# The first gate pair by seven products, with its weights on GpSimd's queue, in a one-layer encoder kernel

## The chip, the cores and the metric

The kernel runs on one core of one Trainium2 chip. The metric is the device time of one execution in microseconds (us). Before the change the median of three runs is 776.86 us, from 776.81 to 778.23. TensorE (PE) multiplies matrices, ScalarE (ACT) and VectorE (DVE) work element by element, GpSimd (POOL) does so too, and issues transfers from its own queue; SyncE (SP) only issues transfers. Each engine takes its instructions strictly in the order in which the program lists them, and an instruction waits on semaphores for what other engines and transfers must have done.

## The reference

One layer over x (512 positions of 1024 features, fp32):

```python
n = rms_norm(h, norm_mix_pre)
proj = n @ w_in                    # columns: gMLP u | gMLP v | q | k | v | gates A, B (1024 each)
y_a = u * (W_s LN(v) + b_s)        # gelu first; 4 chunks of 128 positions, 4 groups of 128 features
y_b = dilated_window_attention(q, k, v)    # 3 patterns x 4 heads, mixed by their denominators
merged = sigmoid(gate_A) * (y_a @ w_branch_a) + sigmoid(gate_B) * (y_b @ w_branch_b)
h = h + rms_norm(merged @ w_out, norm_mix_post)
h = h + rms_norm(relu(rms_norm(h) @ w_up)**2 @ w_down, norm_mlp_post)
```

Everything is fp32. The change lies between y_a and merged @ w_out.

## The kernel before

**Products.** A factor is split into a high part (hi, rounded to the type that TensorE multiplies fast) and a low part (lo, what the rounding left out). One product of 128x128 by 128xN is three matmuls: hi by hi, hi by lo, lo by hi. The usual split is a ScalarE copy for hi and a VectorE subtraction for lo (`wsplit`, L68; `split_into`, L86). The other way is `dma_split` (L78): ScalarE writes hi and then minus hi into the low's tile, and GpSimd issues an accumulating transfer that adds the original weights from memory onto it.

**Seven products.** `seven` and `seven_pairs` (L344 to L390) compute a pair of 128 gate columns for both gates, over 1024 inputs and 512 positions, as a 2x2 block product by seven smaller products instead of eight, each of 12 matmuls of 128x256: 84 matmuls. `seven` forms the sums of the weight blocks on VectorE and splits them; `nmov` holds the sums of the activations, made earlier. The seventh of them, product 4, is deferred as `tail` and stands in the next pair. The same pair written plainly is 2 x 8 products of 128x512, 48 matmuls.

**Stages, in order.** Norm and the V0 projection; V1 and V2; for four heads the q and k projection by seven products and attention (`mix`, heads 0 to 2 store their result to `ybd` in memory, L647); the gMLP: v with LayerNorm per chunk (`evac_v`, L690), and for each of four groups g the u features (`pf`, 24 matmuls of 128x512), the spatial product of that group (`pg`, L727) with the four normalized chunks `vln` and the transposed spatial weights `wst`, and y_a. `prs` (L686) is the sum over `wst` for the LayerNorm bias. `ybh` and `ybl` are loaded back from `ybd` at L659, on GpSimd's queue. LayerNorm's reciprocal root is a power on GpSimd (`rs_out`, L104), one for each chunk, and VectorE applies it (`vln`, L702).

Then the gates and branches, for d from 0 to 7: weights `gw` (1 MB for a pair) and branch weights `bw` (two of 256 KB), gates by sigmoid, then `branches` (L790): y_b by w_branch_b (b1) and y_a by w_branch_a (b0), 12 matmuls of 128x512 each, times the gates, summed, and split into `mh` and `ml`, block d of w_out's input. `GSTD = 1`: pair 0 is written plainly (L802 to L807), pairs 1 to 7 by seven products. After that w_out (`pd`, L849 to L909): its eight blocks k are loaded two at a time (`wow`) into one raw ring of three buffers which the first up weights (`upw`) use next; two pre copies split the first up weights. Then norm, up and down.

**What sets the order.** The code is written stage by stage, but the order of each engine's instructions is set at build time by a scheduler which plays the program through with a cost model of its own and puts what it thinks ready first. So a new buffer or another queue can move instructions that the diff does not name. On a queue nothing overtakes: a transfer that waits holds up all that stands behind it on its engine.

**Memory.** Tiles lie in pools, opened and closed like a stack. A pool that is opened on memory of a closed one waits for that one's last readers. `gpool` holds the gMLP's tiles and `gapool` the gate stage's.

## Time and profile before

| | |
|---|---|
| median of 3 runs | 776.86 us |
| the profiled execution | 776.86 us |
| its span, first to last instruction | 775.1 us |
| mean granted clock of TensorE | 0.999 |
| busy: TensorE, its weight loads, VectorE, ScalarE, GpSimd | 766.0, 691.2, 604.4, 463.9, 88.0 us |
| moved by DMA | 130.40 MB, 168 GB/s in the mean |

Rows of a timeline give the start in us, the duration in us, the engine, the line of the code, the operation and "output<-inputs"; in square brackets stands how long the engine had been idle before and what released it. A matmul's duration is longer than the step to the next one, since matmuls are pipelined; what a matmul costs is the step. In a list of waits the columns are the total, the number and the longest, in us. A row of transfers gives the queue, the number, the size and the median time from issue to landing. A row of stretches gives for each engine its busy time and in brackets its instructions, then TensorE's clock, the share of DMA and GB/s; the engines stand in the order PE, PE's weight loads, DVE, ACT, POOL.

### The profile page before, as it was taken

The numbers are of one execution on the slowest core, as the hardware profiler recorded it, in microseconds if no ns is written. First come the engines' busy times: TensorE is split into PE (matmuls) and PEld (weight loads), VectorE is DVE, ScalarE is ACT, GpSimd is POOL, SyncE is SP. The second block draws the span as 40 slices with busy tenths as digits, with TensorE's granted clock in tenths as the row PEclk, the third lists the DMA queues.
The fourth block names the chain that finished last, engine by engine and source line by source line (L and its number), as shares of the span: only waits on it lengthen the run. The fifth ranks groups of instructions, "written<-read, shape, count | busy, mean of one in ns | idle before, by whom it ended". The sixth has DMA issues, their size and how long they took to land.

```text
span 775.1 us, 12382 instructions
## 1 busy us (share of the span) xinstructions
PE 766.0 (99%) x4859; PEld 691.2 (89%) x4859; DVE 604.4 (78%) x974; ACT 463.9 (60%) x755; POOL 88.0 (11%) x125
## 2 busy tenths in 40 slices
PE   8999999999999999999999999999999999999996
PEld 5888999999998889999998899999999988888885
DVE  7884689888883878768756559998888699978785
ACT  6351468978778545445444457566666766655671
POOL 3310200010103300000000210011211100203010
PEclk9999999999999999999999999999999999999999
DMA  9733743262548933434536324469998998979803
GB/s 310 250 115 109 213 109 110 55 164 82 142 160 154 233 88 84 109 82 120 147 144 217 135 82 136 160 195 290 204 265 221 240 309 313 193 248 216 217 1 109
DMA packets 108910, 130.40 MB, mean 168 GB/s; under 512 B 3330, under 2 KB 79394, under 8 KB 107955
## 3 DMA queue, kind: packets, MB, share of 16 engines
q1 hardware_dynamic: 83920, 83.50, 34.1%
q0 software_dynamic: 24640, 45.70, 25.7%
q8 instruction: 38, 0.62, 0.3%
q10 hardware_dynamic: 290, 0.40, 0.1%
q14 instruction: 22, 0.17, 0.1%
HBM read 119.63 MB, written 26.74 MB: 189 GB/s over the span
## 4 chain that ended last, share of the span: by engine, by line
PE 97%; issue 1%; DMA 0%; DVE 0%; POOL 0%; ACT 0%; POOLq 0%; DVEq 0%; ACTq 0%
PE pacc L1011 13%; PE pg L361 12%; PE pd L1103 6%; PE pd L1102 6%; PE pd L1104 6%; PE pgacc L361 6%; PE ptp L1011 5%; PE pf L93 5%; PE pf L92 5%; PE pf L94 5%; PE pv L94 4%; PE pv L93 4%; PE pv L92 4%; PE pgS L361 3%; PE pd L94 2%; PE pd L92 2%
## 5 line engine op out<-in xcount | busy, mean ns | idle before, releaser
L1103 PE MATMUL pd<-hl,hhl 128*128 128x512 f32 x224 | 87.1, 389 | 0.0
L1104 PE MATMUL pd<-hl,hhl 128*128 128x512 f32 x224 | 87.0, 389 | 0.0
L1102 PE MATMUL pd<-hl,hhl 128*128 128x512 f32 x224 | 84.7, 389 | 0.0
L1011 PE MATMUL pacc<-nt,hl 128*128 128x256 f32 x504 | 66.1, 279 | 0.0
L1011 PEld LDWEIGHTS pacc<-nt,hl 128*128 128x128 f32 x504 | 61.9, 188 | 0.1
L74 ACT ACTIVATE hi<-s 128x1024 fp32r<-128x1024 f32 x32 | 33.8, 1059 | 29.5 <-DVE s L348 7.9
L1104 PEld LDWEIGHTS pd<-hl,hhl 128*128 128x128 f32 x224 | 42.0, 188 | 8.8
L1102 PEld LDWEIGHTS pd<-hl,hhl 128*128 128x128 f32 x224 | 42.0, 188 | 8.8
L1103 PEld LDWEIGHTS pd<-hl,hhl 128*128 128x128 f32 x224 | 42.0, 188 | 8.6
L75 DVE TENSOR_TENSOR lo<-s,hi 128x1024 fp32r<-128x1024 f32 x32 | 39.0, 1223 | 9.8 <-ACT hi L74 9.6
L87 ACT ACTIVATE hl<-s 128x1024 fp32r<-128x1024 f32 x28 | 29.4, 1057 | 26.1 <-DVE s L994 18.8
L88 DVE TENSOR_TENSOR hl<-dnw,hl 128x1024 fp32r<-128x1024 f32 x32 | 38.4, 1221 | 8.3 <-ACT hl L87 8.3
L87 ACT ACTIVATE hl<-dnw 128x1024 fp32r<-128x1024 f32 x32 | 33.0, 1053 | 19.2 <-DMA dnw<-in_w_down_dram 9.9
L1011 PE MATMUL pacc<-n,hl 128*128 128x256 f32 x336 | 44.1, 279 | 0.0
L1011 PEld LDWEIGHTS pacc<-n,hl 128*128 128x128 f32 x336 | 41.3, 188 | 0.0
L361 PE MATMUL pg<-nt,hi 128*128 128x256 f32 x216 | 39.8, 281 | 0.0
L88 DVE TENSOR_TENSOR hl<-s,hl 128x1024 fp32r<-128x1024 f32 x28 | 34.2, 1221 | 5.2 <-ACT hl L87 5.2
L92 PE MATMUL pf<-nh,hi 128*128 128x512 f32 x96 | 38.0, 396 | 0.0
L93 PE MATMUL pf<-nl,hi 128*128 128x512 f32 x96 | 37.7, 392 | 0.0
L94 PE MATMUL pf<-nh,lo 128*128 128x512 f32 x96 | 37.6, 391 | 0.0
L93 PE MATMUL pv<-lo,nh 128*128 128x512 f32 x96 | 37.4, 390 | 0.0
L92 PE MATMUL pv<-hi,nh 128*128 128x512 f32 x96 | 37.3, 395 | 0.0
(386 smaller groups left out, 2269.9 us busy)
## 6 DMA issues: line engine op xcount, KB each, us to landing
upw<-in_w_up_dram SPq DMA_DIRECT2D x16, 1024.0 KB, 6.1
qkw<-in_w_in_dram SPq DMA_DIRECT2D x24, 512.0 KB, 5.2
dnw<-in_w_down_dram SPq DMA_DIRECT2D x12, 1024.0 KB, 6.9
gw<-in_w_in_dram SPq DMA_DIRECT2D x16, 512.0 KB, 5.2
t3d<-in_w_down_dram POOLq DMA_DIRECT2D x8, 1024.0 KB, 8.5
t1d<-in_w_down_dram POOLq DMA_DIRECT2D x8, 1024.0 KB, 9.6
slab<-in_w_in_dram SPq DMA_DIRECT2D x6, 1024.0 KB, 10.6
tsum<-in_w_down_dram POOLq DMA_DIRECT2D x6, 1024.0 KB, 9.7
```

The costliest lines, as they stand in the source:

```text
L74: nc.scalar.activation(hi, raw, AF.Copy)
L75: (sub or nc.vector).tensor_tensor(lo, raw, hi.bitcast(F32), op=ALU.subtract)
L87: nc.scalar.activation(hi, src, AF.Copy)
L88: return sub.tensor_tensor(lo, src, hi.bitcast(F32), op=ALU.subtract)
L92: nc.tensor.matmul(ps, ah, bh, start=start, stop=False)
L93: nc.tensor.matmul(ps, ah, bl, start=False, stop=False)
L94: return nc.tensor.matmul(ps, al, bh, start=False, stop=stop)
L361: nc.tensor.matmul(ps, a[:, j], b[:, j], start=first and not (j or i), stop=(j == KH - 1 and i == 2), skip_group_check=True)
L1011: ins = nc.tensor.matmul(ps, a[:, j], b[:, j], start=first and not (j or m), stop=(j == KH - 1 and m == 2), skip_group_check=True)
L1102: nc.tensor.matmul(ps, ah, bh, start=start, stop=False, skip_group_check=True)
L1103: nc.tensor.matmul(ps, ah, bl, start=False, stop=False, skip_group_check=True)
L1104: return nc.tensor.matmul(ps, al, bh, start=False, stop=stop, skip_group_check=True)
```

## The change

Pair 0 goes through `seven_pairs` as well (`GSTD = 0`). For it the three plain weight blocks (`ar0`, `a12`, `ar1`) are split first, by `dma_split` with their own 256 KB rows of w_in, and its products come in the order 1, 2, 6, 5, 7, 3, so that those that need only plain blocks stand ahead of those that need sums. `gapool` is opened ahead of the close of the gMLP's pool, on the memory of attention, so that its tiles do not share memory with the gMLP's. The loads of `bw` move from SyncE's queue to GpSimd's, and the lows of both branch weights come by `dma_split`: a second ScalarE copy and an accumulating transfer on GpSimd instead of a subtraction on VectorE. `gapool` stays open beyond w_out, whose blocks from k=3 on are split into its tiles, each into one that a gate step has done with: k=3 into `ar0` and `a12`, k=4 into `bw` and `ar1`, k=5 into `b1` and `b0`, k=7's low into `gs`; the pool of w_out's own tiles shrinks from five to three.

```diff
--- before.py
+++ after.py
@@ -75,9 +75,10 @@
         (sub or nc.vector).tensor_tensor(lo, raw, hi.bitcast(F32), op=ALU.subtract)
         return hi, lo
 
-    def dma_split(raw, src):
-        hi = wpool.tile(list(raw.shape), F32R, name="hi", tag="whi")
-        lo = wpool.tile(list(raw.shape), F32R, name="lo", tag="wlo")
+    def dma_split(raw, src, hi=None, lo=None):
+        if hi is None:
+            hi = wpool.tile(list(raw.shape), F32R, name="hi", tag="whi")
+            lo = wpool.tile(list(raw.shape), F32R, name="lo", tag="wlo")
         nc.scalar.activation(hi, raw, AF.Copy)
         nc.scalar.activation(lo, hi.bitcast(F32), AF.Copy, scale=-1.0)
         nc.gpsimd.dma_start(lo, src, accum_op=ALU.add)
@@ -341,14 +342,19 @@
     by_r = perm[:, 2 * P:2 * P + 4].unsqueeze(1).unsqueeze(1)
     by_c = perm[:, 2 * P + 4:2 * P + 8].unsqueeze(1).unsqueeze(3)
 
-    def seven(raw, sums, split2, split1):
+    def seven(raw, sums, split2, split1, first=False):
         raw = raw.rearrange("p (j h) (r c) -> p j (h r) c", h=2, r=2)
+        if first:
+            plain = [split1(raw[:, :, i], tag, i) for i, tag in ((1, "ar0"), (3, "a12"), (2, "ar1"))]
         s = sums()
         nc.vector.tensor_tensor(s[:, :, 0:4:2], raw[:, :, 1:3], raw[:, :, 0:1].to_broadcast([P, KH, 2, P]), op=ALU.add)
         nc.vector.tensor_tensor(s[:, :, 3], s[:, :, 2], raw[:, :, 1], op=ALU.add)
         s12 = split2(s[:, :, 2:4])
-        ar = [split1(raw[:, :, 1], "ar0"), split1(raw[:, :, 2], "ar1")]
-        a12 = split1(raw[:, :, 3], "a12")
+        if first:
+            ar, a12 = plain[::2], plain[1]
+        else:
+            ar = [split1(raw[:, :, 1], "ar0"), split1(raw[:, :, 2], "ar1")]
+            a12 = split1(raw[:, :, 3], "a12")
         nc.vector.tensor_tensor(s[:, :, 1], s[:, :, 3], raw[:, :, 3], op=ALU.add)
         s34 = split2(s[:, :, 0:2])
         pick = lambda g, i: [z[:, :, i] for z in g]
@@ -366,17 +372,22 @@
             c2, c1 = rows(i)
             w = weights(i)
             Y, Z, X = banks()
-            product(6, Y, w, moving, True)
+            p1, z5, u2, u3 = snap("p1", two), snap("z5", 1), snap("u2", 1), snap("u3", 1)
             if tail:
+                product(6, Y, w, moving, True)
                 tail()
             product(1, X, w, moving, True)
-            p1, z5, u2, u3 = snap("p1", two), snap("z5", 1), snap("u2", 1), snap("u3", 1)
             nc.scalar.activation(p1, X, AF.Copy)
+            if not tail:
+                product(2, X, w, moving, False)
+                evac(i, c1[:, A], X)
+                product(6, Y, w, moving, True)
             nc.vector.tensor_tensor(u2, Y, p1, op=ALU.add)
             product(5, Z, w, moving, True)
             nc.scalar.activation(z5, Z, AF.Copy)
-            product(2, X, w, moving, False)
-            evac(i, c1[:, A], X)
+            if tail:
+                product(2, X, w, moving, False)
+                evac(i, c1[:, A], X)
             product(7, Y, w, moving, False)
             nc.vector.scalar_tensor_tensor(u3, Y, -1.0, p1, op0=ALU.mult, op1=ALU.subtract)
             product(3, Z, w, moving, False)
@@ -732,16 +743,16 @@
             split_into(yah[:, g], yal[:, g], tf)
 
     attn.close()
+    gp = ExitStack()
+    gapool = pool(gp, "gapool")
+    gst.close()
     mst = ExitStack()
     mpool = pool(mst, "mpool")
     mh = mpool.tile([P, KD, S], F32R, name="mh")
     ml = mpool.tile([P, KD, S], F32R, name="ml")
-    gp = ExitStack()
-    gst.close()
-    gapool = pool(gp, "gapool")
     gs, rawb = {}, {}
 
-    GSTD = 1
+    GSTD = 0
 
     w7 = w_down.rearrange("(c j h p) d -> c h p j d", p=P, h=2, j=4)
     halves = [slice(0, 512), slice(512, 1024)]
@@ -765,14 +776,23 @@
         raw = wload([KD, 2, P], lambda r: [(r[:, :, 1 - br], fcols(w_in, COL_G + br * D + d * P, KD, P)) for br in range(2)], "gw")
         rawb[d] = gapool.tile([P, 2, 4, P], F32, name="bw")
         for br, w in enumerate((w_branch_a, w_branch_b)):
-            nc.sync.dma_start(rawb[d][:, br], w[:, d * P:(d + 1) * P].rearrange("(k p) c -> p k c", p=P))
+            nc.gpsimd.dma_start(rawb[d][:, br], w[:, d * P:(d + 1) * P].rearrange("(k p) c -> p k c", p=P))
 
         return raw
 
     def gate_weights(i):
         raw = gate_raw(i + GSTD)
+
+        def added(src, tag, blk):
+            hl = gapool.tile([P, 2, KH, P], F32R, name=tag)
+            c0 = COL_G + (1 - blk % 2) * D
+            rows = w_in[:, c0:c0 + P].rearrange("(j h p) c -> h p j c", p=P, h=2)
+            dma_split(src, rows[blk // 2], hl[:, 0], hl[:, 1])
+            return hl[:, 0], hl[:, 1]
+
         with nullcontext() if i else tc.issue_after(normed[-1].ins):
-            return seven(raw.rearrange("p k r c -> p k (r c)"), wsum, wsplit, lambda src, tag: split1(src, tag, gapool))
+            return seven(raw.rearrange("p k r c -> p k (r c)"), wsum, wsplit,
+                         lambda src, tag, blk=0: added(src, tag, blk) if not i else split1(src, tag, gapool), not i)
 
     def gate_banks():
         return [psA.tile([P, 512], F32, name="pg" + tag, tag=tag, bufs=nb)[:, A] for tag, nb in (("acc", 4), ("acc", 4), ("S", 2))]
@@ -791,7 +811,7 @@
         g = gs.pop(d)
         for br in (1, 0):
             bhl = gapool.tile([P, 2, 4, P], F32R, name=f"b{br}")
-            split_into(bhl[:, 0], bhl[:, 1], rawb[d][:, br])
+            dma_split(rawb[d][:, br], fcols((w_branch_a, w_branch_b)[br], d * P, 4, P), bhl[:, 0], bhl[:, 1])
             yh, yl = ((yah, yal), (ybh, ybl))[br]
             pb = feature_tile(bhl[:, 0], bhl[:, 1], 4, yh, yl, "Ty"[br])
             nc.vector.tensor_tensor(g[:, 1 - br], pb, g[:, 1 - br], op=ALU.mult)
@@ -807,7 +827,6 @@
         branches(d)
     seven_pairs(KD - GSTD, gate_weights, nmov, gate_banks, lambda nm, nb: gapool.tile([P, 256], F32, name=nm, bufs=nb), 1,
                 gate_rows, gate_evac, gate_after)
-    gp.close()
     front.close()
     right.close()
 
@@ -849,13 +868,19 @@
             nc.vector.scalar_tensor_tensor(dst[:, hs], ys[hf], r, res[:, hs], op0=ALU.mult, op1=ALU.add)
 
     wo = ExitStack()
-    wopool = pool(wo, "wopool", bufs=5)
+    wopool = pool(wo, "wopool", bufs=3)
+    homes = iter([gapool.tile([P, D], F32R, name="wo", tag=tag) for tag in ("ar0", "a12", "bw", "ar1", "b1", "b0")]
+                 + [wopool.tile([P, D], F32R, name="wo", tag="wo") for _ in range(3)] + [gapool.tile([P, D], F32R, name="wo", tag="gs")])
     accs = [[psB.tile([P, 512], F32, name="pd", tag=tg, bufs=4) for _ in range(2)] for tg in ("acc",) * 4]
     wos, early = [], []
     for k0 in range(0, KD, 2):
         raw = wload([2, D], lambda r: [(r, w_out[k0 * P:(k0 + 2) * P].rearrange("(k p) c -> p k c", p=P))], "wow")
         for j in range(2):
-            wos.append(wsplit(raw[:, j]) if k0 + j < 3 else wsplit(raw[:, j], wopool, tag="wo"))
+            if k0 + j < 3:
+                wos.append(wsplit(raw[:, j]))
+            else:
+                wos.append((next(homes), next(homes)))
+                split_into(*wos[-1], raw[:, j])
     raw = wload([KD, 2 * P], lambda r: [(r, fcols(w_up, 0, KD, 2 * P))], "upw")
     for j in range(2):
         hl = prepool.tile([P, 2, KD, P], F32R, name="pre", tag="pre")
@@ -918,6 +943,7 @@
     wo.close()
     rst.close()
     mst.close()
+    gp.close()
     wstack.close()
 
     wback = pool(back, "wback", bufs=5)
```

The built program has 84 matmuls of 128x256 in the place of 48 of 128x512, 4800 rows of TensorE against 4764. At two places the order changes in a way that the diff does not tell.

GpSimd at the end of attention and the start of the gMLP, before: `rs_out_2949`, `_2963`, `_2977`, `_2991` are the LayerNorm powers of chunks 0 to 3, `lo_3161` and `lo_3207` the accumulating transfers of the u features of groups 2 and 3.

```order
L83 DMA lo_3161<-in_w_in_dram 128x8x128
L104 TENSOR_TENSOR rs_out_2949<-rs_in_2947,neghalf_66 128x1
L659 DMA ybh_2802<-ybd_108 128x3x512
L659 DMA ybl_2803<-ybd_108 128x3x512
L104 TENSOR_TENSOR rs_out_2963<-rs_in_2961,neghalf_66 128x1
L83 DMA lo_3207<-in_w_in_dram 128x8x128
L104 TENSOR_TENSOR rs_out_2977<-rs_in_2975,neghalf_66 128x1
L104 TENSOR_TENSOR rs_out_2991<-rs_in_2989,neghalf_66 128x1
```

The same place of the change, with what follows on GpSimd (`bw_3271` and `bw_3388` are the branch weights of pairs 0 and 1).

```order
L84 DMA lo_3161<-in_w_in_dram 128x8x128
L670 DMA ybh_2802<-ybd_108 128x3x512
L670 DMA ybl_2803<-ybd_108 128x3x512
L105 TENSOR_TENSOR rs_out_2949<-rs_in_2947,neghalf_66 128x1
L105 TENSOR_TENSOR rs_out_2963<-rs_in_2961,neghalf_66 128x1
L105 TENSOR_TENSOR rs_out_2977<-rs_in_2975,neghalf_66 128x1
L84 DMA lo_3207<-in_w_in_dram 128x8x128
L105 TENSOR_TENSOR rs_out_2991<-rs_in_2989,neghalf_66 128x1
L779 DMA bw_3271<-in_w_branch_a_dram 128x4x128
L779 DMA bw_3271<-in_w_branch_b_dram 128x4x128
L84 DMA ar0_3274<-in_w_in_dram 128x4x128
L84 DMA a12_3278<-in_w_in_dram 128x4x128
```

The power of chunk 0 stood ahead of the two loads and stands behind them now; the transfers of the gate stage follow behind the last power, where before there was none. On TensorE the first `pg` stays right behind `prs` and ahead of group 1's u features.

ScalarE at the start of w_out, before: `hi_4596` is the high part of w_out's block 2, the next ones of blocks 3 to 7, `gs_4315` the sum of the last pair.

```order
L74 ACTIVATE hi_4596<-wow_4594 128x1024
L786 ACTIVATE gs_4315<-gs_4315,cols_65 128x256
L787 ACTIVATE gs_4315<-gs_4315,cols_65 128x512
L87 ACTIVATE mh_3259<-gs_4315 128x512
L74 ACTIVATE hi_4600<-wow_4594 128x1024
L74 ACTIVATE hi_4606<-wow_4604 128x1024
L74 ACTIVATE hi_4610<-wow_4604 128x1024
L74 ACTIVATE hi_4616<-wow_4614 128x1024
L74 ACTIVATE hi_4620<-wow_4614 128x1024
L87 ACTIVATE pre_4626<-upw_4624 128x1024
L87 ACTIVATE pre_4629<-upw_4624 128x1024
```

The same place of the change: `hi_4686` is block 2, `wo_4662` and `wo_4664` are blocks 6 and 7 (3 to 5 stand earlier), `gs_4392` the sum of the last pair.

```order
L74 ACTIVATE hi_4686<-wow_4684 128x1024
L806 ACTIVATE gs_4392<-gs_4392,cols_65 128x256
L88 ACTIVATE wo_4662<-wow_4698 128x1024
L88 ACTIVATE wo_4664<-wow_4698 128x1024
L807 ACTIVATE gs_4392<-gs_4392,cols_65 128x512
L88 ACTIVATE pre_4706<-upw_4704 128x1024
L88 ACTIVATE pre_4709<-upw_4704 128x1024
L88 ACTIVATE mh_3263<-gs_4392 128x512
```

The last `mh` stood third behind block 2 and ahead of the other blocks; it stands now behind all blocks and behind both copies of the up weights. On TensorE the first 22 matmuls of w_out, of two banks, use no part of the last `mh`; the 23rd does.

## The prediction

> **What bounds the kernel now.** I read the page's head and its chain first, then the list of waits on TensorE, and after that the timelines of the two places where the order of work changes.
>
> ```profile
> span 775.1 us, 12382 instructions
> PE 766.0 (99%) x4859; PEld 691.2 (89%) x4859; DVE 604.4 (78%) x974; ACT 463.9 (60%) x755; POOL 88.0 (11%) x125
> PE   8999999999999999999999999999999999999996
> ...
> PE 97%; issue 1%; DMA 0%; DVE 0%; POOL 0%; ACT 0%; POOLq 0%; DVEq 0%; ACTq 0%
> ...
> PE pt L200 <- DVE xn L196: 1.6, 2, 1.3
> PE idle L168 <- POOL neghalf L60: 1.0, 1, 1.0
> PE pv L93 <- DVE w0lo L215: 0.2, 1, 0.2
> ```
>
> TensorE is busy for 766.0 of 775.1 us, 97% of the chain is TensorE itself, and the list of its waits has three rows, 2.8 us in all, on lines of the opening norm and V projection. From the first head to the end no matmul waits for anyone. So the time is the sum of the start-to-start steps of the matmuls: a matmul saved is worth its step, and any new wait of TensorE is paid whole. The profiled execution is the median of the runs (776.86 us, 1.8 above its span), so I add to 776.86.
>
> **The matmuls.** The first gate pair's 48 plain 128x512 products run here from the first to the start of the next pair's product; twelve branch matmuls of 128x512, then twelve 128x256 of a seven-product step, run near the end; the last row covers six whole pairs.
>
> ```profile
> 284.40 0.48 PE L92 MATMUL pf<-nh,hi 128*128 128x512 f32 x1
> ...
> 295.38 0.40 PE L361 MATMUL pgacc<-nt,hi 128*128 128x256 f32 x2
> ...
> 403.42 0.28 PE L361 MATMUL pgacc<-nh,hi 128*128 128x256 f32 x1
> ...
> 404.85 0.40 PE L92 MATMUL pf<-yah,b 128*128 128x512 f32 x1
> ...
> 407.60 1.56 PE L361 MATMUL pgacc<-nt,ar 128*128 128x256 f32 x12
> 409.00 0.39 PE L92 MATMUL pd<-hi,mh 128*128 128x512 f32 x1
> ...
> 311.00:405.00 94.00, 94.00 (x650) 87.61 (x649) 68.38 (x107) 44.56 (x78) 0.15 (x2) 1.00 0.42 121
> ```
>
> The 48 take 295.38 - 284.40 = 10.98 us, 0.229 each; twelve of 128x512 take 2.75 us, also 0.229; twelve of 128x256 take 1.43 or 1.40, 0.118 each. Seven products are 84 of the small ones: 84 x 0.118 = 9.9 us. The six pairs give the other bound: 94.0 / 6 = 15.67 us a pair, less 24 x 0.229 = 5.50 for the branches, leaves 10.17 for the 84. The saving is 0.8 to 1.1 us; I take **-0.9**.
>
> **What ScalarE and VectorE gain and lose.** Each branch low loses a VectorE subtraction (0.69 us for 128x512, the ml row below) and gets a second ScalarE copy (0.63, the mh row below) and a GpSimd transfer: 19 copies, 12 us, on ScalarE, about 11 us off VectorE. By the row of six pairs ScalarE works 44.56 and VectorE 68.38 us of 94, so two copies a pair (1.25 of 15.67) fit; I cost them at nothing. The low now takes 0.63 for the copy, then a DMA, against 0.69 before. What hides this is the lead: in the new GpSimd order the b1 low of a pair is issued ahead of the b0 low of the pair before, the better part of 15.67 us early. Without that cover it would cost some us in each of seven pairs.
>
> **First stall: GpSimd at the gMLP.** The change opens the gate pool earlier and hangs new transfers on GpSimd, and the order there is new: both loads of ybh and ybl now stand ahead of the power that makes LayerNorm's scale for chunk 0 (rs_out). What this does is to be seen on chunk 1, which stands behind them already. GpSimd, VectorE and TensorE before:
>
> ```profile
> 257.11 1.25 POOL L104 TENSOR_TENSOR rs_out<-rs_in,neghalf 128x1 f32<-128x1 f32 x1
> 261.78 0.81 POOL L659 DMA_DIRECT2D ybh<-ybd  x1 [3.42 <-DMA ybd<-yb]
> 262.58 0.76 POOL L659 DMA_DIRECT2D ybl<-ybd  x1
> 263.36 0.57 POOL L104 TENSOR_TENSOR rs_out<-rs_in,neghalf 128x1 f32<-128x1 f32 x1
> ...
> 258.39 0.55 DVE L702 TENSOR_SCALAR vln<-vln,mv,rs_out 128x512 f32<-128x512 f32 x1 [0.26 <-POOL rs_out L104]
> ...
> 263.97 0.55 DVE L702 TENSOR_SCALAR vln<-vln,mv,rs_out 128x512 f32<-128x512 f32 x1 [2.54 <-POOL rs_out L104]
> ...
> 262.68 0.38 PE L727 MATMUL pg<-wst,vln 128*128 128x128 f32 x2
> ...
> ybd<-yb POOLq DMA_DIRECT2D x1, 512.0 KB, 7.2
> ...
> ybd<-yb POOLq DMA_DIRECT2D x3, 512.0 KB, 9.0
> ...
> ybd<-yb POOLq DMA_DIRECT2D x1, 512.0 KB, 10.4
> ```
>
> The ybh load waited 3.42 us for the last head's store to ybd to land, at 261.7, and everything behind it on GpSimd waited too: chunk 1's power ran at 263.36 and its vln at 263.97, with VectorE idle for 2.54 us. TensorE did not notice, as it needs chunk 0 first, at 262.68, and that had been normalized at 258.39. Now chunk 0 takes chunk 1's place: power 263.36 to 263.93, vln 263.97 to 264.52, and TensorE's first pg, still in its old place right behind prs, starts at 264.56 instead of 262.68: **+1.9 us**. Queued behind that pg are all matmuls of the second u feature. The last rows are the first store's time to landing, the median of the three, and the last one's, which counts here. GpSimd's order is unchanged up to it, so I keep its 10.4 us; at 9.0 the stall would be 0.5, at 7.2 nothing. Bounds 0 and 1.9. The later chunks move by the same 1.9 on TensorE as on VectorE, so I add nothing for them.
>
> **Pair 0's lows.** The first low (ar0, 256 KB, added by DMA) stands on GpSimd behind the two bw loads of its pair, and these wait for the last py, since the pool lies on attention's old memory.
>
> ```profile
> 268.56 0.39 PE L640 MATMUL py<-ptb,v12s 128*128 128x128 f32 x2
> ...
> 277.25 1.05 PE L727 MATMUL pg<-wst,vln 128*128 128x128 f32 x8
> 278.06 0.48 PE L92 MATMUL pf<-nh,hi 128*128 128x512 f32 x1
> ...
> DMA to landing us min/median/max: 3.2/5.7/7.2
> ...
> DMA to landing us min/median/max: 6.3/8.5/9.9
> ```
>
> The last py ends at 268.95, so at 270.8 with the first stall. Two issues of 0.8 us (as ybh's) put ar0's at 272.4. Product 1 stands in the new order where 278.06 is here, 280.0 with the stall, and needs its low two matmuls on. So 7.8 us are to be had. The nearest rows lie on both sides: plain 256 KB loads of v12s on this queue took 3.2 to 7.2 (first row), accumulating 512 KB loads 6.3 to 9.9 (second). I take 0, as half the bytes should bring it nearer to the first; the bounds are 0 and +2.3. [...]
>
> **Second stall: ScalarE at w_out.** In the new order ScalarE converts the first up weights (two pre copies) ahead of the last mh, and VectorE does pre ahead of ml. Before, mh came first:
>
> ```profile
> 404.93 1.06 ACT L74 ACTIVATE hi<-wow 128x1024 fp32r<-128x1024 f32 x1 [2.26 <-PE pgacc L361]
> ...
> 411.87 0.63 ACT L87 ACTIVATE mh<-gs 128x512 fp32r<-128x512 f32 x1 [1.49 <-DVE gs L798]
> ...
> 422.21 2.02 ACT L87 ACTIVATE pre<-upw 128x1024 fp32r<-128x1024 f32 x2 [4.10 <-DMA upw<-in_w_up_dram]
> ...
> 406.03 1.23 DVE L75 TENSOR_TENSOR lo<-wow,hi 128x1024 fp32r<-128x1024 f32 x1 [0.55 <-ACT hi L74]
> ...
> 412.54 0.69 DVE L88 TENSOR_TENSOR ml<-gs,mh 128x512 fp32r<-128x512 f32 x1 [0.70 <-ACT mh L87]
> 414.35 5.77 DVE L75 TENSOR_TENSOR lo<-wow,hi 128x1024 fp32r<-128x1024 f32 x5 [1.13 <-ACT hi L74]
> ...
> 415.61 0.37 SPq L66 DMA_DIRECT2D upw<-in_w_up_dram  x1
> ...
> upw<-in_w_up_dram SPq DMA_DIRECT2D x1, 1024.0 KB, 6.5
> ...
> DMA to landing us min/median/max: 5.5/6.1/10.8
> ```
>
> I count from the start of ScalarE's hi for w_out's third block (k=2), released by product 3 of the last pair before and after (0 = 404.93). The up load needs the raw buffer of blocks 2 and 3. Its last reader was k=3's low (the load went out at 415.61, as the first of five lows ended); now block 3 is split earlier and the last reader is k=2's low, which ends at 2.33. So the load goes out at 2.4 and, with this load's own 6.5, its copy starts at 9.0 (before, 422.21 - 415.61 = 6.6 after the issue); two pre copies take 2.02, mh 0.63: mh is ready at about 11.55. TensorE began w_out at 4.07 (409.00); two of the twelve b0 matmuls between products 3 and 4 have moved ahead of product 3, so now at 3.61. Ahead of the first matmul that reads the last mh stand 22 of 0.229: it is reached at 8.64. The stall is **+2.9 us**. ml and k=7's low (0.69 + 1.23) have twelve more matmuls (2.7 us) to come in and just do. The last row is the shortest, median and longest of all up loads: 5.5 and 10.8 make stalls of 1.8 and 7.2. I stay with this load's own, though here gain and two x blocks (1.5 MB) go out on GpSimd's queue in the same us. Behind these w_out, the norm and the up stage follow one another unchanged.
>
> **Sum:** -0.9 + 1.9 + 0 + 2.9 = +3.9; 776.86 + 3.9 = **780.8 us**, slower by 0.5%.
>
> **Rivals.** (A) *The store to ybd lands by 259.8.* It need come only 1.9 us sooner, in 8.5 us, for the first stall to be gone; one store of three did. Against it: nothing on any queue changes before it. With the second stall at 1.8 to 2.9 the time is 777.8 to 778.9, half of that no slower than can be told. (B) *Neither wait reaches TensorE,* and its own sum decides: 776.0. It needs the store by 259.8 and also the last mh by 8.64, so the up load within 3.7 us of its issue, or a run of TensorE that gets to w_out later; no row of the up load is that short. This is the only way to a time not above 776.86, by 0.9. (C) *The accumulating low is late.* At 9.9 us ar0 lands 2.1 after TensorE wants it, and a12 and ar1, each an issue of 0.8 later, follow; it decides from 7.8 us on. If besides the up load takes 8 us or more beside gain and x, the second stall is over 4.3: 782 to 785. For it: the two rows of 512 KB; against it: half the bytes.
> [...]
>
> **How the numbers follow.** Forecast 0.52, A 0.14, B 0.14, C 0.20. The forecast's own range is 779.5 to 782; with A's and C's it is 776.4 to 784.5, which leaves out most of B and the end of C. A measurement of this kernel tells about 0.2%, 1.55 us, from no change. Faster than 775.3 could only be B with the largest saving: 0.04. Within 0.2%: the rest of B, half of A and a little of the forecast, 0.20. Slower: 0.76.
>
> **What would show it.** In the new profile TensorE's waits should list a pg of the spatial gating released by VectorE's vln, 1.9 us, with the first rs_out on GpSimd after the ybl load; and a pd that waits on ScalarE's last mh, 2.9 us, with two pre copies right ahead of that mh and idle time for upw ahead of them. The first pair should take 9.9 to 10.2 us of TensorE. A wait of pgS on a DMA into ar would be C; none of these waits, B. Any wait of a branch matmul (pf) on its low, pair after pair, would make the whole argument on cover wrong.

## The result, and the profile after

The changed kernel takes 797.23 us (median of four runs, 795.6 to 798.12) against 777.55 for the kernel before on the same chip: a ratio of 1.0253, with an interval of 1.0241 to 1.0266. It is slower by 2.5% where 0.5% was forecast, 16.4 us above the forecast and outside its range. The profiled execution is the longest of the four, 798.12 us.

The head of the page after, TensorE in the 40 slices of the span, the chain, and GpSimd's queue (packets, MB, share of 16 DMA engines):

```profile
span 796.3 us, 12505 instructions
PE 773.0 (97%) x4895; PEld 696.1 (87%) x4895; DVE 598.1 (75%) x966; ACT 476.8 (60%) x780; POOL 125.1 (16%) x160
PE   9999999999999999998887999999999999999996
...
PE 87%; DMA 7%; issue 2%; DVE 2%; ACT 1%; SPq 1%; POOL 0%; POOLq 0%; DVEq 0%; ACTq 0%
...
q0 software_dynamic: 35952, 54.88, 31.7%
```

The chain is no longer TensorE alone: 7% of it are transfers. The holes are in the 19th to the 22nd slice (358 to 438 us), the gates and the start of w_out. The list of TensorE's waits (total, number, longest) names who releases it:

```profile
PE pf L95 <- DMA b<-in_w_branch_a_dram: 7.8, 4, 3.6
PE pd L93 <- ACT mh L88: 4.1, 1, 4.1
PE pgacc L367 <- DVE u L392: 2.6, 3, 1.5
```

The second row is the forecast's second stall. The first is what the forecast named as its own refutation: branch matmuls that wait for their low, pair after pair. The forecast's first stall, a pg behind vln, is not in the list.

I added up TensorE's start-to-start steps over the median step of each shape, by stage. From 344.5 to 412 us, pairs 3 to 7, the changed kernel loses 15.1 us (before 0.4 there); in w_out 6.4 (before 0); in the opening 0.8 more than before, where the change touches nothing; the matmuls at their usual steps come to 1.0 us less. So 14.7 + 6.4 + 0.8 - 1.0 = 20.9 of the 21.2 us between the two spans. (The medians differ by 19.7: the profiled execution after is the longest of its four, the one before is among the shorter of its own.)

**The gates.** Gate weights and lows landing between 300 and 412 us (number, size, median us to landing), before and after:

```profile
gw<-in_w_in_dram SPq DMA_DIRECT2D x8, 512.0 KB, 5.2
```

```profile
gw<-in_w_in_dram SPq DMA_DIRECT2D x10, 512.0 KB, 8.4
...
b<-in_w_branch_b_dram POOLq DMA_DIRECT2D x7, 256.0 KB, 5.4
...
b<-in_w_branch_a_dram POOLq DMA_DIRECT2D x6, 256.0 KB, 9.4
```

The last row is the low that TensorE's first wait names. The load on SyncE's queue, which the change did not touch, became 3.2 us longer. One turn of the loop over pairs shows what that does. First before: SyncE issues the load, VectorE forms the sum s from it.

```profile
334.70 0.99 SPq L66 DMA_DIRECT2D gw<-in_w_in_dram  x2
340.54 1.23 DVE L347 TENSOR_TENSOR s<-gw 128x1024 f32<-128x1024 f32 x1 [1.39 <-DMA gw<-in_w_in_dram]
347.90 0.63 ACT L87 ACTIVATE ar<-gw 128x512 fp32r<-128x512 f32 x1 [2.52 <-PE pgacc L361]
349.28 1.00 SPq L66 DMA_DIRECT2D gw<-in_w_in_dram  x2
```

The same turn after, from the timelines of the four engines:

```profile
334.68 1.30 SPq L66 DMA_DIRECT2D gw<-in_w_in_dram  x2
...
345.96 1.22 DVE L350 TENSOR_TENSOR s<-gw 128x1024 f32<-128x1024 f32 x1 [7.03 <-DMA gw<-in_w_in_dram]
...
348.81 1.06 ACT L74 ACTIVATE hi<-s 128x1024 fp32r<-128x1024 f32 x1 [8.13 <-DVE s L351]
...
350.18 0.62 ACT L82 ACTIVATE b<-bw 128x512 fp32r<-128x512 f32 x1
350.83 0.63 ACT L83 ACTIVATE b<-b 128x512 fp32r<-128x512 f32 x1
351.37 0.62 ACT L88 ACTIVATE ar<-gw 128x512 fp32r<-128x512 f32 x1
...
351.84 1.29 POOL L84 DMA_DIRECT2D b<-in_w_branch_b_dram  x1 [14.31 <-ACT b L83]
353.42 0.78 POOL L779 DMA_DIRECT2D bw<-in_w_branch_a_dram  x1 [0.29 <-ACT b L82]
...
354.94 1.36 POOL L84 DMA_DIRECT2D b<-in_w_branch_a_dram  x1
...
352.02 0.69 DVE L89 TENSOR_TENSOR ar<-gw,ar 128x512 fp32r<-128x512 f32 x1
...
352.74 2.75 SPq L66 DMA_DIRECT2D gw<-in_w_in_dram  x2
```

Read it as a ring. The load goes out at 334.68; VectorE is idle for 7.03 us and starts s at 345.96, 11.3 us later (before 5.8). ScalarE, idle for 8.13 us, splits s; only then, in its order, come the copies of b and of ar. The b copies let GpSimd, idle for 14.31 us, issue the low; ar's low lets SyncE issue the next load at 352.74. From s to that issue it takes 6.8 us, so a turn keeps TensorE's pace of 15.67 us as long as s comes within 8.9 us of the issue. Before, it came after 5.8, and ScalarE then waited 2.52 us for TensorE before it copied ar: TensorE set the pace. After, the two issues are 18.1 us apart (the turn before took 16.4, the next one 18.6): the load sets it. And all transfers of a pair leave together, within some 4 us (351.84 to 354.94): 1 MB on SyncE's queue, two lows and two plain loads on GpSimd's. From a load's issue to s the DMA engines were about equally busy (before and after; the last two figures of a row are their share and GB/s):

```profile
334.70:340.54 5.84, 5.84 (x51) 5.84 (x50) 4.45 (x7) 3.75 (x7) 0.00 (x0) 1.00 0.90 238
```

```profile
334.68:345.96 11.28, 10.65 (x77) 9.72 (x76) 4.09 (x7) 4.07 (x8) 2.85 (x3) 1.00 0.94 188
```

So s does not wait for idle engines: after, they have packets for twice as long.

**The start of w_out.** The profile after:

```profile
422.50 0.37 SPq L66 DMA_DIRECT2D upw<-in_w_up_dram  x1
...
430.99 2.01 ACT L88 ACTIVATE pre<-upw 128x1024 fp32r<-128x1024 f32 x2 [4.31 <-DMA upw<-in_w_up_dram]
432.90 0.61 ACT L88 ACTIVATE mh<-gs 128x512 fp32r<-128x512 f32 x1
433.57 0.80 PE L93 MATMUL pd<-wo,mh 128*128 128x512 f32 x1 [4.13 <-ACT mh L88]
```

This is the forecast's chain: up load, two pre copies, mh, TensorE. The copy starts 8.5 us after the load's issue, where the forecast had 6.6.

### The profile page after: what moved, and what is told of

It is laid out like the page before. It is cut to its first block, busy times and chain, and to the rows that moved or that the text cites. A ratio compares the mean times of both kernels' runs of the same rounds, so it can differ in the third digit from the quotient of the medians.

```text
span 796.3 us, 12505 instructions
## 1 busy us (share of the span) xinstructions
PE 773.0 (97%) x4895; PEld 696.1 (87%) x4895; DVE 598.1 (75%) x966; ACT 476.8 (60%) x780; POOL 125.1 (16%) x160
## 4 chain that ended last, share of the span: by engine, by line
PE 87%; DMA 7%; issue 2%; DVE 2%; ACT 1%; SPq 1%; POOL 0%; POOLq 0%; DVEq 0%; ACTq 0%
PE pacc L1037 12%; PE pg L367 11%; PE pd L1129 6%; PE pd L1130 6%; PE pd L1128 6%; PE ptp L1037 5%; PE pgacc L367 5%; PE pf L95 3%; PE pf L94 3%; PE pf L93 3%; PE pv L95 3%; PE pv L93 3%; PE pv L94 3%; DMA gw<-in_w_in_dram 3%; DMA xt<-in_x_dram 2%
## 5 line engine op out<-in xcount | busy, mean ns | idle before, releaser
L74 ACT ACTIVATE hi<-s 128x1024 fp32r<-128x1024 f32 x34 | 35.8, 1057 | 56.6 <-DVE s L351 33.4
L75 DVE TENSOR_TENSOR lo<-s,hi 128x1024 fp32r<-128x1024 f32 x34 | 41.5, 1222 | 9.6 <-ACT hi L74 9.3
L95 PE MATMUL pv<-hi,nl 128*128 128x512 f32 x96 | 36.9, 391 | 0.0
L1118 DVE TENSOR_TENSOR hhl<-hid,hhl 128x1024 fp32r<-128x1024 f32 x24 | 29.3, 1221 | 9.2 <-ACT hhl L1117 8.8
L1117 ACT ACTIVATE hhl<-hid 128x1024 fp32r<-128x1024 f32 x24 | 25.2, 1055 | 17.6 <-PE pd L1130 17.6
## 6 DMA issues: line engine op xcount, KB each, us to landing
tsum<-in_w_down_dram POOLq DMA_DIRECT2D x6, 1024.0 KB, 10.1
```

The costliest lines, as they stand in the source:

```text
L74: nc.scalar.activation(hi, raw, AF.Copy)
L75: (sub or nc.vector).tensor_tensor(lo, raw, hi.bitcast(F32), op=ALU.subtract)
L95: return nc.tensor.matmul(ps, al, bh, start=False, stop=stop)
```

## The experiments

The theories. *Traffic:* the accumulating lows keep the DMA engines busy, the gate load beside them comes late, and the ring above turns slower than TensorE. Its rivals: *copies* (the second ScalarE copy of each low is the price), *queue* (the move of bw to GpSimd's queue is), and *latency* (a low by DMA simply comes later than a subtraction, whatever else is under way). For w_out: *order* (pre ahead of mh).

**e1: mh and ml ahead of pre.** The rest of the change is left.

```diff
-        split_into(mh[:, d], ml[:, d], g[:, 0])
+        mlast[:] = [nc.scalar.activation(mh[:, d], g[:, 0], AF.Copy)]
+        mlast.append(nc.vector.tensor_tensor(ml[:, d], g[:, 0], mh[:, d].bitcast(F32), op=ALU.subtract))
...
-        split_into(hl[:, 0], hl[:, 1], raw[:, :, j * P:(j + 1) * P])
+        with tc.issue_after(mlast[0].ins), tc.issue_after(mlast[1].ins):
+            split_into(hl[:, 0], hl[:, 1], raw[:, :, j * P:(j + 1) * P])
```

> Edit: the changed kernel, with the last mh and ml ordered ahead of the two pre copies and their lows; nothing else moves. In the changed kernel (797.2 us) the last mh waits behind the up weights and TensorE loses 4.3 us on it, 0.4 on the next block, and about 1.7 more as its matmuls of 128x512 step by 0.43 us instead of 0.23 for some 4 us after the wait. Theory (ScalarE's order at w_out is one of two separate causes): all 6.4 us come back, 790.8 us, and no wait on mh is left. Rival (the up weights are late anyhow and the wait moves to the up stage): 794 to 797, with a new wait on pre.

792.19 us (1.0187; 1.0168 to 1.0206). The wait on mh is gone, the waits in the gates stay (pf for b 6.9 us, pgacc 2.9). The order is worth 5.0 us beside slow gates, where I had expected 6.4.

**e2: the branch lows by VectorE; e3: bw back on SyncE's queue; e4: both.**

```diff
-            dma_split(rawb[d][:, br], fcols((w_branch_a, w_branch_b)[br], d * P, 4, P), bhl[:, 0], bhl[:, 1])
+            split_into(bhl[:, 0], bhl[:, 1], rawb[d][:, br])
```

```diff
-            nc.gpsimd.dma_start(rawb[d][:, br], w[:, d * P:(d + 1) * P].rearrange("(k p) c -> p k c", p=P))
+            nc.sync.dma_start(rawb[d][:, br], w[:, d * P:(d + 1) * P].rearrange("(k p) c -> p k c", p=P))
```

> Edit: the changed kernel, with both branch lows made by VectorE's subtraction again; the bw loads stay on GpSimd's queue. Theory (the pair's transfers are one burst which the accumulating lows lengthen: 2.0 MB instead of 1.5, so that the gate weights land after 8 to 11 us instead of 5, the sums, the copies and the next load follow late, and the loop over pairs gets longer than TensorE's 15.7 us): the gate stage's 15 us come back, gate weights land in 5.5 to 6.5 us, the wait at w_out stays: 781 to 783 us. Rival (GpSimd's queue with the bw loads is what is late): the branch copies now wait for bw, and 788 or more is left.

> Edit: the changed kernel, with the bw loads on SyncE's queue again; the lows stay accumulating transfers on GpSimd. Theory (volume and kind of the burst): the same bytes in the same burst, so most of the loss stays, 792 to 798 us, with waits of pf on b0's low as before. Rival (the queue: b0's low stands behind two bw issues of 0.8 us each on GpSimd): the waits on b0's low shrink by 1.6 us or more each, 784 to 790.

> Edit: the changed kernel, with both undone: bw on SyncE's queue, branch lows by VectorE. Theory: as with the lows alone, 781 to 783, less at most 0.5; the bw loads' queue is worth nothing by itself. Rival (both parts count): 2 us or more below the run with the lows alone.

e2: 785.62 us (1.0107; 1.009 to 1.0124). e3: 795.91 (1.0238; 1.0222 to 1.0254). e4: 784.74 (1.0094; 1.0079 to 1.0109). The waits on TensorE and GpSimd's queue in e2:

```profile
PE pd L93 <- ACT mh L88: 5.2, 1, 5.2
...
q0 software_dynamic: 27504, 50.69, 28.0%
```

So the lows are the cause: without them 11.6 us are gone and the gates' waits with them. By TensorE's steps from 311 to 412 us, e2 leaves 1.2 of the 14.7 us. *Queue* falls: e3 differs from the changed kernel by 1.3 us, and e4 from e2 by 0.9. e2 came out above the 781 to 783 us that I had expected, in part since the stall at w_out grew: its up load took 9.3 us. e4 missed the same range.

**e5: all three undone together** (the edits of e1, e2 and e3), so that of the change only the seven products of pair 0, with their three accumulating lows, and the pools are left.

```diff
+            nc.sync.dma_start(rawb[d][:, br], w[:, d * P:(d + 1) * P].rearrange("(k p) c -> p k c", p=P))
...
+            split_into(bhl[:, 0], bhl[:, 1], rawb[d][:, br])
...
+        with tc.issue_after(mlast[0].ins), tc.issue_after(mlast[1].ins):
```

> Edit: the changed kernel with all three undone: branch lows by VectorE, bw on SyncE's queue, last mh ahead of pre. What is left of the change is pair 0 by seven products (its three plain lows by accumulating transfers), the buffers apart and reused by w_out. Theory (the two causes add up, and nothing else in the change costs): the wait on mh of 4.4 us and the slow steps behind it are gone, 784.7 - 6.7 = 778.0 or less; with the saving of 0.9 forecast for pair 0 the kernel before would be beaten, 776.3. Rival (something in the buffers or in pair 0 costs what its matmuls save): 777.2 to 778.5.

778.02 us (1.0009; 1.0 to 1.0017). The 19 us are back, the 1.0 of the matmuls is not won, as the rival had it: TensorE still loses 1.3 us in w_out, behind VectorE's lows of w_out's blocks.

**e6: the copies alone.** ScalarE writes both copies, VectorE then makes the low; there is no transfer.

```diff
-            dma_split(rawb[d][:, br], fcols((w_branch_a, w_branch_b)[br], d * P, 4, P), bhl[:, 0], bhl[:, 1])
+            nc.scalar.activation(bhl[:, 0], rawb[d][:, br], AF.Copy)
+            nc.scalar.activation(bhl[:, 1], bhl[:, 0].bitcast(F32), AF.Copy, scale=-1.0)
+            nc.vector.tensor_tensor(bhl[:, 1], rawb[d][:, br], bhl[:, 0].bitcast(F32), op=ALU.subtract)
```

> Edit: the changed kernel with the branch lows by VectorE and bw on GpSimd's queue, but with the second, negated ScalarE copy of each branch weight kept (VectorE's subtraction overwrites it): the ScalarE work of the change without its transfers. Theory (the transfers lengthen the pair's loop, the copies do not): 785 to 786.5, as without the copies. Rival (ScalarE's order: 1.25 us a pair ahead of the copies that release the gate weights' buffer): waits in the gate stage, 788 or more.

784.25 us (1.0094; 1.0078 to 1.0109), not above e2, with no wait in the gates. *Copies* falls; so far the forecast's count of ScalarE was right.

**e7: plain transfers alone.** VectorE makes the lows; GpSimd stores each high part, 256 KB, to memory that nothing reads.

```diff
+    spare = tc.dram_tile([KD, 2, P, 4, P], F32R, name="spare")
...
+            split_into(bhl[:, 0], bhl[:, 1], rawb[d][:, br])
+            nc.gpsimd.dma_start(spare[d, br], bhl[:, 0])
```

> Edit: as e2 (branch lows by VectorE, bw on GpSimd's queue), plus a plain transfer of 256 KB from each branch weight's high part to memory on GpSimd's queue, issued where the accumulating one was; nothing waits for it but the buffer's next use. Theory in its first form (bytes in the burst): gate weights land after 7.5 to 10 us, waits in the gate stage of 3 us or more, 788 to 795. Theory in its second form (an accumulating transfer is dearer than its bytes, or the wait for its landing is what counts): gate weights land in 6 to 7.5 us, 785 to 787.

785.4 us (1.0103; 1.0084 to 1.0122), no wait in the gates. As many transfers on the same queue with as many bytes, and nothing is lost: it has to be something of the accumulating transfer itself: its kind, its pieces (these stores go in pieces of 2 KB, 144 packets more for each on the queue's count than in e2, the lows in pieces of 512 bytes, 528 packets), its latency or its load on the engines.

**e8: e5 without any accumulating low in the gates** (pair 0's three too).

```diff
-                         lambda src, tag, blk=0: added(src, tag, blk) if not i else split1(src, tag, gapool), not i)
+                         lambda src, tag, blk=0: split1(src, tag, gapool), not i)
```

> Edit: as e5, and the three plain lows of pair 0 by VectorE too, so that no accumulating transfer is left in the gate stage. Theory: the lows of pair 0 landed in time in the changed kernel (no wait on them was listed), so no difference from e5 by more than 0.5 us. Rival (they delay something in the first pair): 0.5 to 1.5 us less than e5.

778.17 us (1.0009; 1.0001 to 1.0018), as e5: pair 0's lows by DMA cost nothing and win nothing.

**e9: accumulating transfers that nobody waits for.** As e7, but the store adds onto that memory, in pieces of 512 bytes as the lows have them. **e10:** the same pieces, stored plainly.

```diff
+    spare = tc.dram_tile([KD, 2, P, 4, 2, P], F32R, name="spare")
...
+            split_into(bhl[:, 0], bhl[:, 1], rawb[d][:, br])
+            nc.gpsimd.dma_start(spare[d, br, :, :, 0], bhl[:, 0], accum_op=ALU.add)
```

```diff
+            nc.gpsimd.dma_start(spare[d, br, :, :, 0], bhl[:, 0])
```

> Edit: as e2 (branch lows by VectorE, bw on GpSimd's queue), plus an accumulating transfer of 256 KB in pieces of 512 B from each branch weight's high part to memory that nobody reads, on GpSimd's queue: the kind of transfer that the change brought, but no matmul waits for it. By the queue's share of time an accumulating low of the changed kernel costs about 2.1 us of all 16 DMA engines, a plain 256 KB load 0.85. Theory (the time that accumulating transfers take from the gate weights' loads is the cause): gate weights land after 8 us or more in most pairs and TensorE waits for sums again, 788 to 795. Rival (what counts is that TensorE must wait for the low's own landing): 785 to 786.5, as e2.

> Edit: as e9, the same pieces of 512 B to the same places, but plain instead of accumulating. Theory (the accumulating kind is dear, not the pieces): 785 to 786.5, and the queue's time for these transfers under half of e9's. Rival (pieces of 512 B are dear whatever they do): as e9.

e9: 795.37 us (1.0227; 1.0212 to 1.0243), at the upper end of its theory. e10: 788.61 (1.0145; 1.0131 to 1.0159). The waits of TensorE in e9, VectorE's wait for the gate load from 345 to 412 us, and the landings:

```profile
PE pgacc L367 <- DVE u L392: 7.2, 4, 2.8
...
DVE s L350 <- DMA gw<-in_w_in_dram: 18.7, 3, 6.5
...
gw<-in_w_in_dram SPq DMA_DIRECT2D x10, 512.0 KB, 8.5
spare<-b POOLq DMA_DIRECT2D x13, 256.0 KB, 4.6
```

This settles it between *latency* and *traffic*: no low comes by DMA here, nobody waits for the transfers, and the gate load is as late (8.5 us) and the kernel nearly as slow as with the lows; the wait has only moved from the branches' pf to pgacc, behind VectorE, which waits for the gate load. (ScalarE waited once for a late bw as well, 4.9 us.) What is left open is small: e9 is 1.9 us faster than the changed kernel although its transfers keep the engines longer, and that much may be what the wait for the lows themselves adds. I had expected e10 at 785 to 786.5, so the pieces of 512 bytes carry a part of it by themselves. GpSimd's queue over the whole run in e7, e9 and e10:

```profile
q0 software_dynamic: 29808, 54.88, 29.8%
```

```profile
q0 software_dynamic: 35952, 54.88, 32.6%
```

```profile
q0 software_dynamic: 35952, 54.88, 31.0%
```

A share times its span (796.3 after, 783.1 e2, 781.3 e7, 793.8 e9, 786.2 e10) is the packet time of this queue, spread over 16 engines. Packet times can overlap (from 318.3 to 327.4 us after, the share is 1.05), so these are prices beside this traffic, not for a transfer alone. Less e2's 219.3 us and over 16 transfers, that is the price of one:

| on GpSimd's queue, 16 x 256 KB more than in e2 | packet time over 16 engines, us each | gw to landing, median us | time, us |
|---|---|---|---|
| none (e2) | 0 | 6.1 | 785.62 |
| plain store, 2 KB pieces (e7) | 0.85 | 6.9 | 785.40 |
| plain store, 512 B pieces (e10) | 1.53 | 7.3 | 788.61 |
| accumulating low from memory, 512 B (the change) | 2.07 | 8.4 | 797.23 |
| accumulating store, 512 B (e9) | 2.47 | 8.5 | 795.37 |

(The shares are rounded to 0.1%, 0.05 us each way.) The gate load's delay goes with the engines' time (6.1 us with none of it, 8.5 with 2.47 us a transfer); how the engines divide their time between the two queues, no run shows. The column of landings counts each half of a pair's load from its own issue; what must stay within the ring's 8.9 us is the time from the first issue to s. In the timelines that is at most 8.4 us in the five pairs of e7 issued from 304 to 367 us, which lose nothing; one of five is over 9 us in e10 (10.4), four in e9 (9.4 to 10.9), and after they take 8.9 to 12.0.

**e11: one low of each pair by DMA, the other by VectorE.**

```diff
+            if br:
+                dma_split(rawb[d][:, br], fcols((w_branch_a, w_branch_b)[br], d * P, 4, P), bhl[:, 0], bhl[:, 1])
+            else:
+                split_into(bhl[:, 0], bhl[:, 1], rawb[d][:, br])
```

> Edit: the changed kernel with the low of b0 by VectorE again and the low of b1 still by an accumulating transfer. b1's low is issued ahead of the pair's gate weights, b0's behind them. Theory (the pair's transfers and its loop must together stay under TensorE's 15.7 us; one low of 2.1 us less): gate weights land after 6 to 8.5 us, most of the gate stage's loss is gone, 785.5 to 789. Rival (each low costs its half): 790.5 to 792.

787.31 us (1.0133; 1.0119 to 1.0148), the gate load at 6.6 us, one wait of pf for a low, 1.6 us: half of the lows cost 1.7 us over e2, both cost 11.6. That is nearer to a threshold than to a price per transfer: only one of its pairs has s later than 8.9 us after the issue (10.8). But e11 keeps the low that leaves ahead of the pair's gate load and drops the one behind it, and no run does the reverse, so the place of the low may have a part in it.

**e12: e5 with w_out's blocks in other tiles,** to see whether the rest in w_out came from block 4's low waiting for its tile.

```diff
-    homes = iter([gapool.tile([P, D], F32R, name="wo", tag=tag) for tag in ("ar0", "a12", "bw", "ar1", "b1", "b0")]
-                 + [wopool.tile([P, D], F32R, name="wo", tag="wo") for _ in range(3)] + [gapool.tile([P, D], F32R, name="wo", tag="gs")])
+    homes = iter([gapool.tile([P, D], F32R, name="wo", tag=tag) for tag in ("ar0", "a12", "bw")]
+                 + [wopool.tile([P, D], F32R, name="wo", tag="wo")] + [gapool.tile([P, D], F32R, name="wo", tag=tag) for tag in ("b1", "b0")]
+                 + [wopool.tile([P, D], F32R, name="wo", tag="wo") for _ in range(2)] + [gapool.tile([P, D], F32R, name="wo", tag=tag) for tag in ("ar1", "gs")])
```

> Edit: e5 with the low of w_out's block k=4 in a tile of w_out's own pool instead of ar1's, which product 4 of the last pair frees, and k=7's high part in ar1's instead. In e5 TensorE waited 0.4 us at k=4 and 0.5 later at the start of w_out (1.3 with small steps beside it), which is more than pair 0 saves. Theory (the buffers' reuse costs what the products save): 0.4 to 1.2 us less than e5, 776.3 to 777.5, at or just under the kernel before. Rival: no difference from e5, as the waits are VectorE's own amount of work there.

779.56 us (1.0032; 1.0021 to 1.0042). Its wait:

```profile
PE pd L93 <- ACT mh L819: 1.3, 1, 1.3
```

This is 1.5 us slower than e5, so neither expectation gave the number. The low came earlier, and the wait went to mh: VectorE now makes three lows of w_out (3.49 us) ahead of the last pair's sum instead of two (2.35). What binds is how much VectorE has to do ahead of that sum, not the tile, which was the rival's reason.

**e13: e5, with three banks of w_out begun ahead** (k = 0 to 2 of the first three, 27 matmuls that need neither the last mh nor a late block). **e14:** the same without pair 0's accumulating lows (e8's edit).

```diff
...
+    begun = [(0, 0), (0, 1), (1, 0)]
+    for n, (t, hf) in enumerate(begun):
+        with tc.issue_after(final.ins) if n else nullcontext():
+            final = out_part(t, hf, range(3))
...
+            with tc.issue_after(final.ins):
+                final = out_part(t, hf, range(3 if (t, hf) in begun else 0, KD))
```

> Edit: e5, with TensorE beginning w_out on three banks with blocks k=0 to 2 (27 matmuls), as the kernel before does, and coming to blocks 3 to 7 behind them; in e5 and in the changed kernel it goes through blocks 0 to 6 of one bank first, and waits there for VectorE's lows (0.4 us at k=4, 0.5 at k=7, about 1.3 with the slower steps). Theory (pair 0's 1.0 us is saved and given back at the start of w_out, where the reuse of the gate tiles let the scheduler turn to blocks whose lows are not yet made): no wait in w_out, 776.0 to 776.9, under the kernel before by about 0.9. Rival (e5 is as fast as it can be, its 0.7 over the kernel before comes from somewhere else): 777.5 or more with no wait listed in w_out.

> Edit: e13 with pair 0's three plain lows by VectorE as well, so that no accumulating transfer is left behind the gMLP. Theory: no wait is left for it to take away, so as e13 within 0.5 us, 776.3 to 777.2. Rival (the lows in pair 0 cost something that e13 hides): 775.5 to 776.2.

e13: 776.79 us (0.9993; 0.9984 to 1.0002). e14: 777.46 (1.0; 0.9991 to 1.0009). Before, on that chip: 777.09 and 777.07. e14 missed its theory's range by 0.3 us. No wait is left between the gates and the norm behind w_out. With all waits of the change gone, its seven products are worth at most a few tenths; neither can be told from the kernel before.

**e15: the first stall, on e13.** The forecast's first stall had failed to come; the reading was that SyncE's gate load for pair 1 had moved out of the store's way. Rows of the timelines before, and after with the store's own row (us to landing):

```profile
246.00 1.06 ACT L81 ACTIVATE hi<-uw 128x1024 fp32r<-128x1024 f32 x1 [0.28 <-PE pv L94]
247.09 1.25 SPq L66 DMA_DIRECT2D gw<-in_w_in_dram  x2
```

```profile
259.50 1.06 ACT L82 ACTIVATE hi<-uw 128x1024 fp32r<-128x1024 f32 x1
260.58 1.22 SPq L66 DMA_DIRECT2D gw<-in_w_in_dram  x2
260.65 0.77 POOL L670 DMA_DIRECT2D ybh<-ybd  x1 [2.12 <-DMA ybd<-yb]
...
262.80 0.55 DVE L713 TENSOR_SCALAR vln<-vln,mv,rs_out 128x512 f32<-128x512 f32 x1 [1.43 <-POOL rs_out L105]
...
ybd<-yb POOLq DMA_DIRECT2D x1, 512.0 KB, 8.5
```

The load takes another raw buffer now, that of a later u feature, and goes out at 260.58 instead of 247.09; the store to ybd, issued at 251.6, lands after 8.5 us instead of 10.4. Vln follows at 262.80, and TensorE's pg does not wait. The test brings 1 MB on SyncE's queue back at 247 us, as stores that nothing reads, and holds the power's place behind the loads of ybh and ybl:

```diff
-        nc.gpsimd.dma_start(carry[z][:, :NH - 1], ybd[:, :, z])
+        loaded = nc.gpsimd.dma_start(carry[z][:, :NH - 1], ybd[:, :, z])
...
-        r = rstd_of(mv[:, 1:2], 1.0, 4.0 * EPS)
+        with tc.issue_after(loaded.ins):
+            r = rstd_of(mv[:, 1:2], 1.0, 4.0 * EPS)
...
+            if g == 1:
+                idle_copy = tc.dram_tile([2, P, KD, 2, P], F32, name="idle_copy")
+                for z in range(2):
+                    nc.sync.dma_start(idle_copy[z, :, :, 0], wh.bitcast(F32))
```

> Edit: e13 with two transfers of 512 KB in pieces of 512 B, from the high part of group 1's u weights to memory that nobody reads, on SyncE's queue at 247 to 248 us, where the kernel before has the 1 MB of pair 1's gate weights and the changed kernel has nothing (it loads them at 260.6, into the buffer that ScalarE's copy of the next u weights frees then); the orders of TensorE and GpSimd are those of e13. Theory (the store to ybd took 10.4 us in the kernel before because of that load, and 7.0 to 8.6 in all runs of the changed order, which is why the first predicted stall did not come): the store lands after 9.5 us or more, the first pg waits 0.7 to 2 us for chunk 0's vln, 777.5 to 779. Rival (the store's time has to do with something else): under 9 us, no wait, as e13.

778.78 us (1.0027; 1.0015 to 1.0039), 2.0 above e13. Its store, its ybh load and its pg:

```profile
261.61 0.77 POOL L670 DMA_DIRECT2D ybh<-ybd  x1 [3.72 <-DMA ybd<-yb]
...
ybd<-yb POOLq DMA_DIRECT2D x1, 512.0 KB, 10.1
...
PE pg L743 <- DVE vln L714: 1.4, 1, 1.4
```

With 1 MB beside it the store takes 10.1 us (7.0 to 8.8 in all other runs of the changed order), and the forecast's stall appears, 1.4 us on TensorE.

## Why the prediction was wrong

**The matmuls: right.** 0.9 forecast, 1.0 measured: the 48 at 0.227 us are 10.9, the 84 at 0.118 are 9.9.

**What ScalarE and VectorE gain and lose: here the forecast failed,** by 14.7 us, most of its error. The step costed the new work at nothing, since the lows are issued the better part of a pair ahead and the engines had time. Both statements held at first: e6 shows that the copies cost nothing, and up to 344 us TensorE waits for no low. What it left out is the other resource that the lows use. I had counted engines' busy time and the lead of a single transfer, not the time that 16 accumulating transfers keep on the DMA engines (2.07 us each by the queue's share, against e2), and not the ring in which the gate load's landing decides when the next low can leave. The lead was no independent cover: it shrank with the very delay that it was to hide. The profile before had the two numbers for it: the load's 5.2 us, and 2.52 us of ScalarE waiting for TensorE in a turn, which is most of the slack that the ring had (5.8 of the 8.9 us were used). What an accumulating 256 KB takes was not in it; the rows of 512 KB at 6.3 to 9.9 us, read as latency, would have been a warning if read as load.

**First stall: it did not come.** The chain of waits was right (e15 makes it appear), but the sentence "GpSimd's order is unchanged up to it, so I keep its 10.4 us" looked at one queue only. The load on SyncE's queue that stretched the store had moved behind it. Rival A described the result, while its argument against itself, that nothing on any queue changes before the store, was what was false. The forecast's 1.9 was 0.

**Pair 0's lows: right.** Issue to landing was 4.9 us in the median of two and 5.6 for the third, within the 7.8 to be had, and TensorE did not wait for them; this half of rival C did not come, the late up load did. One figure of the step was off without an effect on the sum: 9.9 less 7.8 is a bound of 2.1, not 2.3.

**Second stall: right in its mechanism, mis-sized.** The term was 2.9 and measured 6.4. Of that, 1.4 is the stall itself, 4.3 us instead of 2.9 over the usual step, since the load's own 6.5 us were taken from a row with less beside it (8.5 to the copy; from issue to copy the DMA engines moved 185 GB/s before and 287 after; no run tests this by itself). 0.4 is block 4's low. The rest is a thing that the forecast had no term for, the clock, in the last section. e1 and e5 against e4 price the order at 5.0 and 6.7 us.

So the sum that came out is -1.0 + 14.7 + 0 + 0 + 6.4, and 0.8 in the opening, where it was to be -0.9 + 0 + 1.9 + 0 + 2.9. Why the kernel gains nothing even without any stall (e13, e14: spans of 775.0 and 774.9, before 775.1) stays partly open: in both a wait of the opening for its first small load was longer than in the profile before (2.3 and 1.7 us), by TensorE's steps the opening lost 0.8 and 0.7 us more than before, which takes up the saving in these two executions, and the medians agree to a few tenths. Whether the opening does so in every execution, no run shows.

## What to carry to other kernels

A transfer has a price on the DMA engines beside its latency (here 2.07 us of all 16 for a low that landed after 5.4 or 9.4 us in the median): before moving work from an engine to an accumulating transfer, add up what each queue keeps on the engines and ask which other load shares them. Where loads, copies and buffers form a ring, compare the ring's turn with the pace of the engine that is to stay busy; a lead inside the ring is no cover for a delay of the ring (here a turn of 16.4 us became one of 18.1). And a duration taken from the trace holds only as long as what ran beside it, on the other queues too, stays where it was (the store to ybd took 10.4 us before, 8.5 after, 10.1 in e15).

## What the runs showed that I had not expected

Two stalls of TensorE cost more than their length. After the waits of 3.6 and 4.1 us in the profile after, the clock was half, and matmuls of 128x512 stepped by 0.427 us instead of 0.227, for 5.3 and 3.2 us: 2.5 and 1.6 us on top of the waits.

Shorter waits brought it too, but not all of them. Behind 2.35 us of waiting, at 383.73 in the profile after, the steps stayed at 0.227; behind 2.40 us in e3 they were 0.427, and 0.9 us after the end of a wait of 2.81 us in e9 the steps of 128x256 went from 0.118 to 0.213. What parts them is not the length alone. In the profile after, the granted clock changes only on a grid of 3.41 us, and the stretch at half clock shown from e3 is as long: half from 402.60 to 409.43 and from 433.32 to 436.73 in the profile after, from 402.14 to 405.55 in e3. Stretches of that grid, first of the profile after (around 383.73, then around the wait of 3.6 us), then of e3 (busy time and instructions of TensorE, its weight loads, VectorE, ScalarE, GpSimd; then the granted clock, the share of DMA and GB/s):

```profile
382.12:385.53 3.41, 1.80 (x7) 1.24 (x7) 2.13 (x3) 0.12 (x1) 0.00 (x0) 1.00 0.03 5
385.53:388.94 3.41, 2.71 (x20) 2.50 (x20) 3.41 (x8) 2.29 (x4) 0.00 (x0) 1.00 0.00 0
...
399.19:402.60 3.41, 1.37 (x7) 0.90 (x5) 0.97 (x1) 1.36 (x3) 0.39 (x1) 1.00 1.03 282
402.60:406.01 3.41, 1.89 (x5) 1.53 (x6) 0.00 (x0) 0.00 (x0) 0.93 (x1) 0.50 0.61 78
```

```profile
398.73:402.14 3.41, 1.31 (x6) 0.75 (x4) 0.48 (x1) 0.40 (x1) 0.00 (x0) 1.00 1.06 373
402.14:405.55 3.41, 3.10 (x10) 2.72 (x11) 0.00 (x0) 0.86 (x2) 1.29 (x1) 0.50 0.03 11
```

From 344 to 440 us of the profile after, two stretches of the grid were followed by a first one at half clock, and in them TensorE was idle for 2.0 and 3.4 us; those at full clock with 0.9, 1.3, 1.5 and 1.6 us were not. (The stretch from 402.60, with 1.5 us idle and itself at half clock, was followed by another at half.) In e3 a stretch with 2.1 us idle was followed by half clock. The wait of 2.35 us lay across two stretches, with at most 1.6 us in one of them; that of 2.40 had 2.1 us in one. In the opening a shorter wait may have done it: e14, with one wait of 1.7 us there and no other above 1.0, had a mean clock of 0.997, e8, with none above 1.0, 0.999. That is 1.6 us of clock over the span, about one stretch at half, so 2 us need not be the limit everywhere. My estimate, from the 2.5 and 1.6 us above, is that a stall of more than about 2 us may cost some 2 us more, by where it falls; that place was not chosen in any run.
